# Transfers that sum weight blocks hang on ScalarE's convolutions, four raw weight buffers, first activations split in the up projection, six chunks held

## The chip, the cores and the metric

The kernel runs as one program on one core of a Trainium2 chip. The time is device microseconds (us) of one execution, and less is better. A difference between kernels is read from the medians of several executions; where a profile is discussed, the time of that one profiled execution is given beside its span, which runs from the first to the last instruction.

A core has five instruction streams that run side by side and wait for one another through semaphores: TensorE (PE; its weight loads are the row PEld), VectorE (DVE), ScalarE (ACT), GpSimd (POOL) and SyncE (SP). Each runs its instructions in order. Transfers are issued by SP, ACT or POOL, each with a queue of its own, and carried out by 16 DMA engines that all queues share. In the profile q1 is SP's queue, q10 ACT's and q0 POOL's.

## The reference

One layer of an encoder on x of 512 x 1024 float32, in three parts, each between two RMS norms and added to the residual: token mixing (an attention group and a recurrent group, HGRN2), cross-attention into 256 memory rows, and a gated MLP with a convolution over three neighbouring positions. Cut to what the change touches:

```python
def conv_ffn(h, w_up, conv_w, conv_b, w_down):
    n = h.shape[1]
    u = h @ w_up                                  # 512 x 1024 @ 1024 x 5632
    up = jnp.pad(u, ((0, 0), (1, 1), (0, 0)))
    acc = conv_b
    for j in range(3):
        acc = acc + up[:, j:j + n] * conv_w[j]
    gate, val = jnp.split(acc, 2, axis=-1)
    return (jax.nn.silu(gate) * val) @ w_down     # 512 x 2816 @ 2816 x 1024

h = rmsnorm(x, pre_ffn_g)
x = x + rmsnorm(conv_ffn(h, w_up, conv_w, conv_b, w_down), post_ffn_g)
```

## The kernel before

**Precision.** Every float32 operand is split into two parts of a shorter format: `hi`, a cast made by ScalarE, and `lo`, the rest, `source - hi`. A product is three matmuls (`mm3`, L176 to L178): hi by hi, hi by lo, lo by hi. For the weights the parts are `wh` and `wl`.

**Weights.** All weights but those of the down projection lie in DRAM as 110 units of 128 x 1024 (512 KB), in the order in which they are used. `load_w` (L132) takes the next of two buffers `raw` and lets SP load it (L136 for these units, L141 for the down projection's). `issue` (L145) then makes `wh` and `wl`, in four buffers each: normally by a cast on ScalarE (L111) and a subtraction on VectorE (L112). For 35 units of the first half, `wl` is made as a negated copy of `wh` (ScalarE L155 or POOL L157) to which POOL adds the weights by an accumulating transfer from DRAM (L158). Up to three units are issued ahead of the one in use (`AHEAD`). One unit serves 24 matmuls of 512 columns in a projection.

**Down projection.** It is a product of 2 x 2 blocks: tokens 0 to 255 and 256 to 511 against even and odd chunks of 128 features, by two halves of the output columns. Seven block products (`PRODUCTS`) take the place of eight; each has 11 chunks, two row blocks and three matmuls a chunk, so 66 matmuls of 512 columns, and reads 6 weight units (the last of half width). Three of its weight operands are blocks of `w_down` as they stand (`in_wd`: w11, w22, w21), the other four are sums of blocks (`SUMS`: t1, t3, t2, t4). The sums are made in DRAM by transfers alone: `new_sums` (L926) copies a block into a tensor `sum_t` (L930) and adds another to it by an accumulating transfer (L931). t2 is built on t1, and t4 on t2. There are six groups `u` of 1024 columns (the last 512), so 6 x 4 x 2 = 48 transfers, all on POOL's queue. The order of the products is w11, t2, t1, w22, t3, t4, w21.

The activations have sums too. `acts[g]` holds the gated activations of group `g` (chunks 0 to 3, 4 to 7, 8 to 10) as an even and an odd tile; `group_sides` (L934) makes the differences `sides[g]` and turns one half of the even tile into a difference, and `left_side` (L982) splits the operand of product `p` and group `g` into `hi` and `lo`. For group 1 of the products 1 to 6 (`NEG_GROUP`) `lo` is made by POOL and an accumulating transfer (L993, L994), otherwise by VectorE. `lay_ahead` keeps three groups prepared ahead (`LAY_AHEAD`).

**Large tiles.** `b8` is a pool of 16 tiles of 8 KB a partition, given out by `big`: x, the activations, the sides, the left sides and the gains (`gains`, L187) all come from it. A tile is handed to the next owner when its last reader is done.

**The up projection.** It runs over 22 feature blocks `i` and the two halves `c` (gate, value); `conv` (L943) computes the convolution of each: ScalarE L946, VectorE L947 and L949, SiLU on ScalarE (L952) for the gates, the gating product on VectorE (L957). `new_sums(u)` is called behind blocks 2, 5, 8, 11, 14 and 17.

**What sets the order.** The code is written in one sequence, and a scheduler then orders the instructions of each engine by priority and estimated readiness. An instruction that waits for nothing may so be ordered far ahead of its place in the code; `tc.issue_after(ins)` puts an instruction behind `ins` on the same engine. The order is fixed when the kernel is built.

**Start.** Four units against all of x (L407) come first while x and its transposed copy are loaded. ScalarE's squares of x (L420) give the row norms, POOL turns them into a power (L194, L195), and the units from L176 on follow. The recurrent group's output norm is again ScalarE, POOL L195, VectorE L593, PE L597.

Of the kernel before, what the change touches and what calls it, by code (L numbers as in the profile page):

```python
# [9 lines left out]
F32 = mybir.dt.float32  # L10
# [8 lines left out]
P = 128  # L19
# [15 lines left out]
NEG_GROUP = frozenset((p, 1) for p in range(1, 7))  # L35
# [45 lines left out]
def layer(tc, io, out):  # L81
# [49 lines left out]

    def load_w():  # L132
        raw = rawp.tile([P, 1024], F32, name="raw", tag="raw")
        i = issued[0]
        if i < N_WHOLE:
# [787 lines left out]
    acts, sides, gates = [], [], {}  # L923
    half_t = [slice(0, 256), slice(256, 512)]

    def new_sums(u):  # L926
        n = width(u).stop - width(u).start
        for out_name, first_name, second_name in SUMS:
            t = dram.tile([P, n], F32, name="sum_%s_%d" % (out_name, u), tag="sum_%s_%d" % (out_name, u))
            nc.gpsimd.dma_start(t, weight_block(first_name, width(u)))  # L930
# [11 lines left out]

    def conv(c, i, u):  # L943
# [36 lines left out]
    g_post, = gains("post_ffn_g")  # L980

    def left_side(p, g):  # L982
        n = GROUPS[g][1] - GROUPS[g][0]
        even, odd = acts[g]
        if p == 3:
            nc.vector.tensor_sub(sides[g][:, 1, :n], odd[:, :n, half_t[0]], sides[g][:, 1, :n])
        src = (even[:, :n, half_t[0]], sides[g][:, 1, :n], sides[g][:, 0, :n], sides[g][:, 1, :n],
               even[:, :n, half_t[1]], odd[:, :n, half_t[1]], odd[:, :n, half_t[0]])[p]
        t = big([P, 2, 4, 256], F32R)
        hi, lo = t[:, 0, :n], t[:, 1, :n]  # L990
        if (p, g) in NEG_GROUP:
            nc.scalar.copy(hi, src)  # L992
            nc.gpsimd.tensor_scalar(lo, hi.bitcast(F32), -1.0, 0.0, op0=ALU.mult, op1=ALU.add)  # L993
            nc.gpsimd.dma_start(lo, src, accum_op=ALU.add)  # L994
        else:
            split(hi, lo, src)
        return hi, lo

    order = [(p, g) for p in range(7) for g in range(3)]
    laid = {}  # L1000

    def lay_ahead(i):
        while len(laid) < min(len(order), i + LAY_AHEAD):
            laid[order[len(laid)]] = left_side(*order[len(laid)])
# [162 lines left out]
```

## Time and profile before

| | us |
|---|---|
| median of three executions (lowest, highest) | 923.49 (922.62, 924.53) |
| the profiled execution, its own time | 924.11 |
| its span | 922.3 |
| PE busy | 840.2, 91% of the span |
| VectorE busy | 533.1, 58% |
| ScalarE busy | 457.5, 50% |
| POOL busy | 143.6, 16% |

How to read the views: a group of instructions is named by line, engine, operation and `out<-in`, with buffer numbers left out. Behind `|` stands the idle time of the engine just before it, with what ended that idle time. In a timeline the columns are start, duration, engine, line, operation, and in brackets the idle time before it and its releaser. In the view of waits stand the engine and line that waited, what it waited for, the total in us, how often, and the longest. PE's matmuls are pipelined, so the spacing of their starts says more than their durations.

### The profile page before, as it was taken

How to read it: one execution, taken by the hardware profiler on the slowest of the kernel's cores; microseconds unless marked ns; L12 is line 12 of the kernel's file. 1: busy time of each engine (PE TensorE's matmuls, PEld its weight loads, DVE VectorE, ACT ScalarE, POOL GpSimd, SP SyncE). 2: the span in 40 equal slices, each digit the busy share in tenths (PEclk: the TensorE clock that was granted, in tenths of full speed). 3: DMA queues.
4: the chain of work that ended last, by engine and by line, in shares of the span. 5: the costliest groups of instructions: out<-in, count | busy, mean ns of one | idle time of the engine just before them, and what ended most of it. 6: DMA issues, size and time to landing. Idle time of an engine off the chain costs nothing.

```text
span 922.3 us, 11153 instructions
## 1 busy us (share of the span) xinstructions
PE 840.2 (91%) x4238; PEld 701.4 (76%) x4238; DVE 533.1 (58%) x800; ACT 457.5 (50%) x766; POOL 143.6 (16%) x209
## 2 busy tenths in 40 slices
PE   7683977999999999999999999999999996987884
PEld 5472766888989988888888898888888885865663
DVE  2232434773998677584453665556556557555554
ACT  3354355563879887464453554333433343454431
POOL 2141324111442320120000310000000000112011
PEclk9887898999999999999999999999999998999998
DMA  9999998746595763234222143232222332569453
GB/s 291 349 271 288 261 286 193 154 92 137 134 212 134 161 137 143 87 114 137 81 81 69 46 137 115 92 106 99 92 92 92 115 91 58 162 180 210 138 165 126
DMA packets 40198, 136.69 MB, mean 148 GB/s; under 512 B 5136, under 2 KB 7184, under 8 KB 39952
## 3 DMA queue, kind: packets, MB, share of 16 engines
q1 hardware_dynamic: 25632, 86.03, 27.5%
q0 software_dynamic: 13216, 47.19, 24.2%
q10 hardware_dynamic: 1296, 2.76, 0.8%
q8 instruction: 33, 0.54, 0.2%
q14 instruction: 21, 0.17, 0.1%
HBM read 130.72 MB, written 25.17 MB: 169 GB/s over the span
## 4 chain that ended last, share of the span: by engine, by line
PE 67%; DMA 16%; DVE 6%; issue 5%; POOL 3%; ACT 3%; SPq 0%; POOLq 0%; DVEq 0%; ACTq 0%
PE ps_b L178 8%; PE ps_b L177 7%; PE ps_b L176 7%; DMA sum_t<-in_wd_dram 5%; PE ps_s L176 4%; PE ps_s L178 4%; PE ps_s L177 4%; PE ps_o L176 4%; DMA raw<-sum_t 4%; PE ps_o L177 4%; PE ps_o L178 4%; PE ps_c L176 3%; PE ps_c L177 3%; PE ps_c L178 3%; DMA big<-in_x_dram 3%
## 5 line engine op out<-in xcount | busy, mean ns | idle before, releaser
L112 DVE TENSOR_TENSOR wl<-raw,wh 128x1024 fp32r<-128x1024 f32 (+1 forms) x113 | 134.3, 1190 | 177.5 <-ACT wh L111 177.2
L111 ACT CAST wh<-raw 128x1024 fp32r<-128x1024 f32 (+1 forms) x113 | 115.7, 1024 | 197.2 <-PE ps_b L177 53.3
L176 PE MATMUL ps_b<-big,wh 128*128 128x512 f32 (+1 forms) x320 | 120.2, 376 | 6.5 <-ACT wh L111 5.8
L178 PE MATMUL ps_b<-big,wl 128*128 128x512 f32 (+1 forms) x320 | 118.2, 369 | 0.0
L177 PE MATMUL ps_b<-big,wh 128*128 128x512 f32 (+1 forms) x320 | 117.9, 369 | 0.0
L176 PEld LDWEIGHTS ps_b<-big,wh 128*128 128x128 f32 x320 | 61.6, 192 | 16.2 <-ACT wh L111 6.2
L177 PE MATMUL ps_s<-wl,big 128*128 128x512 f32 (+1 forms) x140 | 55.7, 398 | 17.8 <-DMA wl<-in_w_dram 17.2
L178 PEld LDWEIGHTS ps_b<-big,wl 128*128 128x128 f32 x320 | 61.1, 191 | 10.4 <-DVE wl L112 0.8
L177 PEld LDWEIGHTS ps_b<-big,wh 128*128 128x128 f32 x320 | 61.5, 192 | 9.3
L569 DVE TENSOR_TENSOR big<-big 128x512 f32<-128x512 f32 x64 | 48.4, 761 | 32.9 <-PE ps_c L543 25.8
L176 PE MATMUL ps_s<-wh,big 128*128 128x512 f32 (+1 forms) x140 | 55.2, 398 | 2.0 <-ACT wh L111 1.6
L178 PE MATMUL ps_s<-wh,big 128*128 128x512 f32 (+1 forms) x140 | 55.1, 394 | 0.0
L993 POOL TENSOR_SCALAR big<-big 128x1024 fp32r<-128x1024 f32 x6 | 6.3, 1054 | 290.6 <-ACT big L992 290.6
L153 ACT CAST wh<-raw 128x1024 fp32r<-128x1024 f32 x35 | 36.8, 1050 | 27.5 <-PE ps_o L178 11.4
L177 PEld LDWEIGHTS ps_s<-wl,big 128*128 128x128 f32 x140 | 27.7, 198 | 24.0 <-DMA wl<-in_w_dram 18.1
L112 DVE TENSOR_TENSOR big<-ps_o,big 128x512 fp32r<-128x512 f32 x54 | 37.1, 688 | 13.4 <-ACT big L111 13.1
L176 PE MATMUL ps_b<-wh,big 128*128 128x512 f32 x92 | 38.7, 424 | 5.9 <-ACT wh L111 3.4
L178 PE MATMUL ps_b<-wh,big 128*128 128x512 f32 x92 | 38.0, 415 | 4.6 <-DVE big L112 4.6
L176 PE MATMUL ps_o<-wh,big 128*128 128x512 f32 (+1 forms) x102 | 39.5, 392 | 2.9 <-ACT wh L111 2.9
L158 POOL DMA_DIRECT2D wl<-in_w_dram x35 | 33.3, 969 | 54.2 <-ACT wl L155 38.3
L204 POOL TENSOR_SCALAR small<-small 128x1 f32<-128x1 f32 x41 | 17.9, 436 | 152.1 <-ACT tmp L235 133.0
L111 ACT CAST big<-ps_o 128x512 fp32r<-128x512 f32 x54 | 31.7, 587 | 19.4 <-PE ps_o L891 7.5
(266 smaller groups left out, 2074.8 us busy)
## 6 DMA issues: line engine op xcount, KB each, us to landing
raw<-in_w_dram SPq DMA_DIRECT2D x109, 512.0 KB, 3.2
wl<-in_w_dram POOLq DMA_DIRECT2D x35, 512.0 KB, 6.1
sum_t<-in_wd_dram POOLq DMA_DIRECT2D x30, 512.0 KB, 9.9
raw<-sum_t SPq DMA_DIRECT2D x20, 512.0 KB, 3.3
raw<-in_wd_dram SPq DMA_DIRECT2D x15, 512.0 KB, 4.0
sum_t<-sum_t POOLq DMA_DIRECT2D x10, 512.0 KB, 7.5
big<-in_x_dram SPq DMA_DIRECT2D x8, 512.0 KB, 14.7
big<-big POOLq DMA_DIRECT2D x6, 512.0 KB, 5.6
```

The lines of the kernel that those rows point to most:

```text
L111: nc.scalar.copy(hi, src)
L112: (eng or nc.vector).tensor_sub(lo, src, hi.bitcast(F32))
L153: nc.scalar.copy(wh, raw)
L158: nc.gpsimd.dma_start(wl, io["w"][i], accum_op=ALU.add)
L176: nc.tensor.matmul(o, a[0], b[0], start=start, stop=False)
L177: nc.tensor.matmul(o, a[0], b[1], start=False, stop=False)
L178: last_mm[0] = nc.tensor.matmul(o, a[1], b[0], start=False, stop=stop).ins
L204: nc.gpsimd.tensor_scalar(ss[:, i + 4:i + 5], ss[:, i:i + 1], 1.0 / D, ss[:, i + 3:i + 4] if i else EPS, op0=ALU.mult, op1=ALU.add)
L569: nc.vector.tensor_tensor(out=c, in0=c, in1=pat(tt, toff + off, [[2, npair], [gap, 2], [0, m]]), op=ALU.mult)
L993: nc.gpsimd.tensor_scalar(lo, hi.bitcast(F32), -1.0, 0.0, op0=ALU.mult, op1=ALU.add)
```

## The change

It has six parts.

1. In `new_sums`, the first transfer of t1 and of t3 (a plain copy of `in_wd`) is issued by ScalarE, and behind the last SiLU before it in the code (`last_act`). POOL keeps the copies for t2 and t4 and the 24 accumulating transfers.
2. `load_w` takes the down projection's units in turns of four: two into the buffers `raw`, two into the halves of a `big` tile (`raw_room`).
3. `left_side` and `lay_ahead` move ahead of `conv`; the split of product 0, group 0 is called behind the value half of block 8, and three groups are laid before `group_sides(2)`.
4. `NEG_GROUP` loses the products 1 and 3: VectorE makes `lo` of group 1 there.
5. The gains `post_ffn_g` are no tile of their own; they are read into the unused fourth chunk of group 2's tiles, and `out_part` takes the place of `residual_part` in the down projection.
6. `last = NP - 6`: of the last product six chunks, not four, are computed first for row block 0 and then for row block 1, so their four weight units are held.

```diff
-NEG_GROUP = frozenset((p, 1) for p in range(1, 7))
+NEG_GROUP = frozenset((p, 1) for p in (2, 4, 5, 6))
...
+    def raw_room(i):
+        k = (i - N_WHOLE) % 4
+        if i < N_WHOLE or k < 2:
+            return rawp.tile([P, 1024], F32, name="raw", tag="raw")
+        if k == 2:
+            spare[0] = big([P, 2, 1024])
+        return spare[0][:, k - 2, :]
...
-            nc.gpsimd.dma_start(t, weight_block(first_name, width(u)))
+            if first_name in sums:
+                nc.gpsimd.dma_start(t, weight_block(first_name, width(u)))
+            else:
+                with tc.issue_after(last_act[0]):
+                    nc.scalar.dma_start(t, weight_block(first_name, width(u)))
             nc.gpsimd.dma_start(t, weight_block(second_name, width(u)), accum_op=ALU.add)
...
-            nc.scalar.activation(a, a, ACT.Silu)
+            last_act[0] = nc.scalar.activation(a, a, ACT.Silu).ins
...
+                if i == 16:
+                    for c2 in range(2):
+                        nc.gpsimd.dma_start(acts[2][c2][:, 3, :], rows_bc(io["post_ffn_g"][half(c2)], 512))
...
-            if i % 8 == 7 or i == NF - 1:
+            if i % 8 == 7:
                 group_sides(i // 8)
+            if i == 8:
+                lay_ahead(1)
...
+    lay_ahead(3)
+    group_sides(2)
...
-    last = NP - 4
+    last = NP - 6
...
-                lay_ahead(3 * p + j // 4)
+                lay_ahead(3 * p + j // 4 + LAY_AHEAD)
```

**POOL at the start.** POOL's order before, a piece in the token mixing; `sum_t` are the sums with their group and number, L158 a remainder `wl`, L194 and L195 a row norm's power:

```order
L931 DMA sum_t_4_5764<-in_wd_dram 128x1024
L930 DMA sum_t_5_5992<-in_wd_dram 128x512
L930 DMA sum_t_5_5995<-in_wd_dram 128x512
L930 DMA sum_t_4_5767<-sum_t_4_5764 16x8192
L158 DMA wl<-in_w_dram 128x1024
L194 TENSOR_SCALAR small<-small 128x4
L931 DMA sum_t_5_5992<-in_wd_dram 128x512
L195 TENSOR_TENSOR small<-small,nhalf 128x4
```

The same piece of POOL's order now (the lines have moved by ten: L168, L204 and L205 are the old L158, L194 and L195):

```order
L205 TENSOR_TENSOR rx<-rx,nhalf 128x4
L462 CAST masks<-tmp_296 128x896
L168 DMA wl<-in_w_dram 128x1024 x8
L204 TENSOR_SCALAR small<-small 128x4
L205 TENSOR_TENSOR small<-small,nhalf 128x4
```

Before, all 48 sums stand between POOL's first instruction and the recurrent group's first output; now none does, and the orders of PE, ScalarE and SP are the same up to the up projection.

**POOL and ScalarE in the up projection.** POOL's order before, behind the last row norm of the cross-attention:

```order
L204 TENSOR_SCALAR small<-small 128x1 x2
L207 TENSOR_TENSOR small<-small,nhalf 128x1
L189 DMA big<-in_post_ffn_g_dram 128x1024
L993 TENSOR_SCALAR big<-big 128x1024
L994 DMA big<-big 128x1024
```

POOL's order now at that place, the whole of group 0 and the first transfer of group 1 (4840 is t1, 4843 t3, 4846 t2, 4849 t4):

```order
L217 TENSOR_TENSOR small<-small,nhalf 128x1
L945 DMA sum_t_0_4840<-in_wd_dram 128x1024
L945 DMA sum_t_0_4843<-in_wd_dram 128x1024
L941 DMA sum_t_0_4846<-sum_t_0_4840 16x8192
L945 DMA sum_t_0_4846<-in_wd_dram 128x1024
L941 DMA sum_t_0_4849<-sum_t_0_4846 16x8192
L945 DMA sum_t_0_4849<-in_wd_dram 128x1024
L945 DMA sum_t_1_5068<-in_wd_dram 128x1024
```

ScalarE's order now behind the SiLU of block 2 (L992), with the two plain copies L944 of group 0:

```order
L992 ACTIVATE tmp_4799<-tmp_4799 128x512
L944 DMA sum_t_0_4840<-in_wd_dram 128x1024
L986 ACTIVATE tmp_4835<-ps_s,cw 128x512
L944 DMA sum_t_0_4843<-in_wd_dram 128x1024
L111 CAST wh<-raw 128x1024 x2
```

The groups follow one another on POOL, each behind its copies on ScalarE; within a group four transfers form a chain (t1's addition, t2's copy, t2's addition, t4's copy).

**SP around the down projection.** SP's order before, where the weight units of the up projection end (L136) and those of the down projection begin (L141):

```order
L136 DMA raw<-in_w_dram 128x1024 x64
L141 DMA raw<-in_wd_dram 128x1024 x5
L141 DMA raw<-in_wd_dram 128x512
L141 DMA raw<-sum_t_0_4846 128x1024
L141 DMA raw<-sum_t_1_5074 128x1024
L141 DMA raw<-sum_t_2_5308 128x1024
```

SP's order now at the same place (L146 and L151 are the old L136 and L141; `big` is half of a spare tile):

```order
L146 DMA raw<-in_w_dram 128x1024 x58
L151 DMA big<-in_wd_dram 128x1024 x2
L146 DMA raw<-in_w_dram 128x1024 x6
L151 DMA raw<-in_wd_dram 128x1024 x3
L151 DMA raw<-in_wd_dram 128x512
L151 DMA big<-sum_t_0_4846 128x1024
L151 DMA big<-sum_t_1_5074 128x1024
L151 DMA raw<-sum_t_2_5311 128x1024
```

The third and fourth unit of the down projection are loaded ahead of six units of the up projection. Later in SP's order some loads into spare tiles stand ahead of loads into `raw` that are used before them, for example those of t4's first two groups between those of t3's.

More of the change, by code (lines that the diff above doesn't have):

```diff
@@ L130, in width @@
         return slice(u * 1024, min(u * 1024 + 1024, NP * 512))
+    spare = [None]
+    def raw_room(i):
[5 more added lines that the diff above has]
+        return spare[0][:, k - 2, :]
     def load_w():
-        raw = rawp.tile([P, 1024], F32, name="raw", tag="raw")
         i = issued[0]
+        raw = raw_room(i)
         if i < N_WHOLE:
@@ L978, in layer, with out_part @@
             new_sums(i // 3)
[L980 to L1004, printed above, removed]
+    def out_part(ss, y, i, cols, last, tag="ta"):
+        n = cols.stop - cols.start
+        yg = tmp2(tag=tag)[:, :n]
+        nc.scalar.activation(yg, y, ACT.Square, accum_out=ss[:, i:i + 1])
+        rstd_part(ss, i, last)
+        g0 = cols.start % 512
+        nc.vector.tensor_mul(yg, y, acts[2][cols.start // 512][:, 3, g0:g0 + n])
+        return yg, cols
+    lay_ahead(3)
+    group_sides(2)
     def products(y, p, j, w, b):
@@ L1047, in layer @@
                 nc.vector.tensor_add(c12, y[b], v2[b])
-                parts[b].append(residual_part(rows[b], c12, g_post, 0, half(1), False, "th"))
+                parts[b].append(out_part(rows[b], c12, 0, half(1), False, "th"))
         elif p == 4:
@@ L1052, in layer @@
                 nc.vector.tensor_add(v2[b], y[b], v2[b])
-                parts[2 + b].append(residual_part(rows[2 + b], v2[b], g_post, 0, half(1), False))
+                parts[2 + b].append(out_part(rows[2 + b], v2[b], 0, half(1), False))
         elif p == 5:
```

30 lines of the change are left out of this document (26 added, 4 removed).

## The prediction

> **What bounds the kernel now.** I read the busy time by stage first, cut where the other views change. Columns: stretch, its length, each engine's busy us and count, granted TensorE clock, DMA share, GB/s.
>
> ```profile
> core 0: us, PE busy (x) PEld busy (x) DVE busy (x) ACT busy (x) POOL busy (x), PEclk, DMA share, GB/s
> 0.00:48.40 48.40, 31.46 (x104) 23.66 (x104) 11.40 (x18) 16.93 (x27) 10.53 (x22) 0.89 0.99 322
> 48.40:143.00 94.60, 65.87 (x308) 53.36 (x308) 33.46 (x61) 41.47 (x65) 30.37 (x39) 0.82 0.99 269
> 143.00:770.00 627.00, 624.29 (x3363) 533.64 (x3364) 401.17 (x626) 335.42 (x593) 81.63 (x123) 1.00 0.42 116
> 770.00:908.00 138.00, 115.12 (x451) 88.31 (x450) 81.15 (x85) 62.09 (x75) 18.44 (x20) 0.93 0.56 159
> 908.00:922.30 14.30, 3.42 (x15) 2.46 (x14) 5.88 (x12) 1.63 (x6) 2.64 (x5) 0.74 0.20 74
> ```
>
> From 143 to 770 TensorE is busy 624.29 of 627 us: there is nothing to win there, only to lose. It idles 16.9 us before 48.4, 28.7 us up to 143 and 22.9 us in the down projection (770 to 908). In the two early stages the DMA engines are full (0.99). So I asked what PE waits for in the first 160 us, and what POOL waits for there (us in total, times, longest).
>
> ```profile
> PE ps_s L177 <- DMA wl<-in_w_dram: 17.2, 2, 11.0
> PE ps_c L597 <- DVE tmp L593: 11.0, 1, 11.0
> PE ps_s L407 <- ACT wh L383: 9.8, 3, 5.1
> PE ps_b L176 <- ACT wh L111: 5.8, 1, 5.8
> ...
> POOL sum_t L930 <- DMA sum_t<-in_wd_dram: 64.8, 11, 11.5
> ```
>
> POOL issues the weight remainders `wl` (L158) and computes the small power (L195), and it stands 64.8 us in front of transfers that only the down projection needs, 600 us later. Its timeline shows this at the last long wait:
>
> ```profile
> 138.73 0.51 POOL L930 DMA_DIRECT2D sum_t<-sum_t  x1 [9.94 <-DMA sum_t<-in_wd_dram]
> ...
> 141.12 1.39 POOL L195 TENSOR_TENSOR small<-small,nhalf 128x4 f32<-128x4 f32 x1
> ```
>
> L597's 11.0 us are this wait, since DVE L593 needs L195. Before 48.4 the sums take transfer time instead. The queues of 0 to 45 us (packets, MB, share of the 16 engines), two groups of issues (count, KB, median us to landing), and ScalarE's last square of x:
>
> ```profile
> q0 software_dynamic: 1633, 7.21, 57.4%
> q1 hardware_dynamic: 2316, 6.96, 41.2%
> ...
> sum_t<-in_wd_dram POOLq DMA_DIRECT2D x11, 512.0 KB, 9.7
> ...
> sum_t<-sum_t POOLq DMA_DIRECT2D x4, 512.0 KB, 6.8
> ...
> 46.29 1.06 ACT L420 ACTIVATE tmp<-big 128x1024 f32<-128x1024 f32 x1 [1.35 <-DMA big<-in_x_dram]
> ```
>
> In the down projection the bound is another: SP cannot issue a weight load before VectorE has released one of two raw buffers. SP's wait of 770 to 910, and PE's longest one there, at the stage's start:
>
> ```profile
> SPq L141 <- DVE wl L112: 90.4, 37, 11.9
> ```
>
> ```profile
> PE ps_b L178 <- DVE big L112: 4.6, 1, 4.6
> ```
>
> Two loads into one buffer that follow each other in the chain of work (start, us):
>
> ```profile
> 816.31 3.63 DMA raw<-sum_t
> ...
> 822.30 5.12 DMA raw<-sum_t
> ```
>
> One turn of a buffer (load 3.63, cast, subtraction) is 6.0 us, so 2.4 us beside the load; two buffers give a unit every 3.0 us, more where a load takes 5.1.
>
> **The change part by part**, against the profiled execution, 924.11 us (span 922.3 and 1.8 around it; the median of the runs, 923.49, is 0.6 lower, which I leave uncorrected).
>
> *Start, 0 to 48.4.* The changed order issues no sum there. What is left, q1's 6.96 MB, took 41.2% of 45 us, so 18.5 us of all engines; with some 4 us for issue and latency (estimated from the 3.63 of one load) x and the first weights are in by about 23 us instead of 46.3. Then PE's own 96 matmuls bind: 96 x 0.227 (the spacing below) is 22 us from its first at 5 us, and about 5 us more at the low clock: the stage ends near 32. **Gain 16.4**; bounds 8 (half the idle comes back) and 19 (the low clock costs half).
>
> *48.4 to 143.* POOL now holds `wl` issues and small operations alone, so the waits for `wl` (17.2) and L597's 11.0 go: with 0.5 of small ones the stage's 28.7. Each long wait also leaves the matmuls slow for a while:
>
> ```profile
> 93.62 0.80 PE L177 MATMUL ps_s<-wl,big 128*128 128x512 f32 x1 [10.96 <-DMA wl<-in_w_dram]
> ...
> 98.48 0.63 PE L176 MATMUL ps_o<-wh,big 128*128 128x512 f32 x1
> 98.91 0.43 PE L177 MATMUL ps_o<-wl,big 128*128 128x512 f32 x1
> 99.18 0.39 PE L178 MATMUL ps_o<-wh,big 128*128 128x512 f32 x1
> 99.41 0.40 PE L176 MATMUL ps_o<-wh,big 128*128 128x512 f32 x1
> ```
>
> For 5.3 us they start 0.43 apart, then 0.23: twelve matmuls lose 0.2 each, 2.4 us. For the four waits of 5.8, 6.2, 11.0 and 11.0 us I take 2 us each, 8 in all. Late next are the chain cast, negate, `wl` transfer and VectorE's recurrence, which now have 37 us less; I keep 5.7 us for them. **Gain 31**; bounds 20 and 37.
>
> *Up projection (inside 143 to 770).* Twelve plain copies are now issued by ScalarE and the other 36 transfers by POOL, which had nothing to do there. ScalarE's share is low enough (335 of 627 us) that twelve issues cost nothing; without that cover, 12 x 0.5 (the 0.51 of POOL's issue, the nearest row) is 6 us. A weight load now shares the engines. Its price, from a stretch where a load also ran beside POOL's transfers (260 to 340 us, medians again):
>
> ```profile
> wl<-in_w_dram POOLq DMA_DIRECT2D x13, 512.0 KB, 5.5
> raw<-in_w_dram SPq DMA_DIRECT2D x12, 512.0 KB, 3.2
> ```
>
> PE takes a unit each 24 x 0.227 = 5.45 us, two raw buffers allow a turn of 10.9, so a load may take 8.5 us before PE waits; 3.2 is far from it. I take **a loss of 2** for bunched transfers; bounds 0 and 20 (rival B). The first activations, split inside the up projection and not after it, save the stage's first wait (4.6, on the subtraction of that group, and 2.4 at the low clock) and cost a cast and a subtraction in covered time.
>
> *Down projection.* 7 products x 66 matmuls x 0.227 is 105 us. Busy is 115, so 10 are lost to the low clock and 22.9 idle. Four raw buffers halve the supply to 1.5 us a unit (at loads of 5.1: 1.9), below PE's 12 x 0.227 = 2.7, so PE becomes the bound. Late next: VectorE, with two more subtractions of two left sides (1 us each) and 81 of 138 us busy, would be near 75% of the shorter stage; and the two added buffers come from the pool of left sides, so SP's queue, in order, can stand before a slot that PE frees. For these I keep 9 of the 33 us. **Gain 24**; bounds 7 (A) and 33.
>
> Whether the 10 us follow the waits is weighed here. After a wait of only 1.6 us in this stage a matmul soon lasts 0.63 too, as in the slow stretch above:
>
> ```profile
> 854.48 0.73 PE L176 MATMUL ps_s<-wh,big 128*128 128x512 f32 x2 [1.58 <-ACT wh L111]
> ...
> 858.06 0.63 PE L176 MATMUL ps_s<-wh,big 128*128 128x512 f32 x1
> ```
>
> So I let short waits cause low clock, and it goes with them; the other reading is rival E. The Trainium skill, "TensorE: Matmul & The Clock Gate", section "Part 1: The HAM clock gate (the "warmup" mystery)", says that the clock falls after an idle window of about 3.4 us. By it only the stage's longest waits would lower the clock, and E would hold; this row disagrees.
>
> *End.* Six chunks instead of four are computed for one half before the other: 1.4 us more between the two tails, so the first tail no longer meets the second. The stage of 14.3 us is a chain; I take 0, bounds -1 and +2. The gains row read into spare activation slots changes one transfer in covered time: 0, bounds -1 and +1.
>
> Sum: 16.4 + 31 - 2 + 24 + 0 = 69.4; 924.1 - 69.4 = **855**.
>
> **The rivals.**
>
> A, *the end keeps its stalls*: slots of the pool come free no faster than PE works, and SP's order behind them makes the four buffers act as two. For it: loads into the new buffers stand in SP's queue ahead of loads needed sooner. Then only the first wait and its clock (7 of 33) are gained: 16.4 + 31 - 2 + 7 = 52, 872.
>
> B, *weight loads slow in the up projection.* Three queues now run at once on engines that one loads alone today. If a load took three times as long, 9.6 us, a turn would be 12.0 and a unit 6.0: 0.55 over PE's, times 36 units under the sums 20 us, 18 beyond the 2 above: 873. Against it: the 3.2 beside POOL's transfers. The Trainium skill, "DMA: Bandwidth & Descriptors", section "Queues, rings and completion order", has each DMA engine go round its queues packet by packet, which would make that threefold time the limit; the trace shows no doubling with one other queue.
>
> C, *the sums come late*, the one that ends slower. POOL now works one group's chain in a row: two adding transfers and two copies wait for one another, 2 x 9.7 + 2 x 6.8 and six issues of 0.5, 36 us a group at the full engines' medians. New groups come each 6 x 5.45 = 32.7 us; the last one at 770 - 8 x 5.45 = 726, and its second sum is needed near 800 less 8 for load and split. With c for a group, and 0.8c for the last group up to its second sum, PE waits 5 x (c - 32.7) + 0.8c - 66: from c = 40 on, and over 69 us, the whole gain, from c = 52 on. For it: 36 is near 40. Against it: those medians come from engines 99% taken. At c = 55 the time is 944.
>
> D, *the start frees less*: behind the sums stands the next wait (casts, the raw loads), and half of 47 comes: 878.
>
> E, *the down projection's low clock is not its short waits'*: then the wait of 4.6 us stands for 2.4 of the 10, and 7.6 stay: 863. Against it: the rows at 854 to 858.
>
> That the sums would still run early is ruled out by the order: they hang on the activations.
>
> **How the numbers follow.** Forecast 855 (838 to 868): 0.57. A 872 (866 to 884): 0.17. B 873 (864 to 895): 0.09. D 878: 0.07. E 863: 0.03. More than the forecast, all 14.7 us kept back regained, under 838: 0.04. C: 0.03. The range 838 to 884 takes in the forecast, A, E, most of B and D; its lower end is the sum with what is kept back regained. A measurement of this kernel tells 0.2% from no change: faster 0.96, same 0.01 (C near its break-even), slower 0.03.
>
> **What would show it.** Right: no sum on POOL before the up projection; no PE wait for `wl` or L593; the end of the first stage near 32 and L597 near 95; PE without waits in the up projection, with loads under 8.5 us; the down projection's 462 matmuls in about 114 us. Wrong: PE waiting on casts behind `raw` in the up projection (B), a wait for `sum_t` in the second product (C), SP waiting on PE in the down projection (A), or the early stages idle behind another engine (D).

## The result, and the profile after

| | before | after |
|---|---|---|
| median of four executions, us (lowest, highest) | 924.01 (922.62, 924.99) | 828.05 (826.70, 828.51) |
| ratio to before (95% interval) | | 0.896 (0.8944 to 0.8976) |
| the profiled execution, us (its span) | 924.11 (922.3) | 828.14 (826.4) |

The changed kernel is faster by 96.0 us in the profiled executions; 69.4 were forecast (855). The measured time lies below the forecast's range of 838 to 884. The direction and the stages were right, and so, for the most part, was what PE had waited for. The forecast gain was too small in every stage.

First the busy time by stage of the changed kernel, cut at the same places in the program as before: the end of the first stage, L607 (before L597), the up projection's last matmul and the down projection's last. Columns as in the prediction.

```profile
core 0: us, PE busy (x) PEld busy (x) DVE busy (x) ACT busy (x) POOL busy (x), PEclk, DMA share, GB/s
0.00:28.10 28.10, 26.54 (x105) 21.32 (x106) 15.16 (x27) 17.60 (x29) 2.40 (x9) 1.00 0.86 294
28.10:87.80 59.70, 58.37 (x310) 48.83 (x309) 31.48 (x58) 39.22 (x63) 10.43 (x15) 1.00 0.74 195
87.80:713.10 625.30, 622.61 (x3365) 532.41 (x3364) 401.61 (x624) 338.57 (x597) 101.28 (x150) 1.00 0.57 151
713.10:818.30 105.20, 105.12 (x464) 86.60 (x462) 81.97 (x89) 60.05 (x74) 15.96 (x18) 1.00 0.64 195
818.30:826.40 8.10, 0.28 (x2) 0.00 (x0) 3.66 (x8) 0.91 (x4) 1.34 (x3) 0.79 0.35 131
```

PE is now busy to within 3 us in each of the first four rows, and the clock column is 1.00 in all of them. The down projection's 105.12 us are what 462 matmuls take at the warm spacing of 0.227 (104.9): nothing is left of its waits or its low clock. VectorE is busy 82 of 105 us there, 78%, and PE loses nothing by it. The DMA share of the two early stages fell from 0.99 to 0.86 and 0.74; in the long middle row it rose from 0.42 to 0.57 without a cost.

The last two cuts of the kernel before, at the same places (the prediction had cut at 770 and 908; the wait before the first matmul is part of the stage):

```profile
770.10:911.10 141.00, 118.12 (x464) 90.67 (x463) 81.88 (x86) 62.81 (x77) 18.44 (x20) 0.93 0.55 155
911.10:922.30 11.20, 0.32 (x2) 0.00 (x0) 5.14 (x10) 0.91 (x4) 2.64 (x5) 0.66 0.25 94
```

So the gains by stage, in us:

| stage | before | after | gain | forecast (bounds) |
|---|---|---|---|---|
| first stage | 48.4 | 28.1 | 20.3 | 16.4 (8, 19) |
| up to L597 / L607 | 94.6 | 59.7 | 34.9 | 31 (20, 37), with the next row's part |
| from there to the down projection | 627.1 | 625.3 | 1.8 | -2 for the sums (-20, 0) |
| down projection | 141.0 | 105.2 | 35.8 | 24 (7, 33) |
| end | 11.2 | 8.1 | 3.1 | 0 (-1, +2) |

The 1.8 us of the third row are the slow matmuls behind L597's wait of 11 us, which the prediction had counted in the second stage; that stage's gain is 36.7. Between 188 and 770 us the distance of the two kernels stays at 57 us: the sums cost the up projection nothing.

PE's waits over the whole changed kernel (us in total, times, longest), the four largest:

```profile
PE ps_b L378 <- DVE tmp L359: 1.3, 1, 1.3
PE ps_s L187 <- DMA wl<-in_w_dram: 0.9, 1, 0.9
PE ps_b L186 <- DVE big L112: 0.8, 1, 0.8
PE ps_b L661 <- ACT big L662: 0.7, 2, 0.5
```

Of the 17.2 us for `wl` 0.9 are left, L607 does not stand here at all, and none of these waits lies in the up or the down projection. Transfers of the middle stretch (count, KB, median us to landing):

```profile
raw<-in_w_dram SPq DMA_DIRECT2D x93, 512.0 KB, 3.4
sum_t<-in_wd_dram POOLq DMA_DIRECT2D x20, 512.0 KB, 8.1
...
sum_t<-sum_t POOLq DMA_DIRECT2D x10, 512.0 KB, 4.6
```

A weight load takes 3.4 us, far from the 8.5 at which rival B would begin.

### The profile page after: what moved, and what is told of

Same layout as the page of the kernel before. It is cut to its first block, busy times and chain, and to the rows that moved or that the text cites. A ratio compares the mean times of both kernels' runs of the same rounds, so it can differ in the third digit from the quotient of the medians.

```text
span 826.4 us, 11158 instructions
## 1 busy us (share of the span) xinstructions
PE 812.9 (98%) x4238; PEld 689.2 (83%) x4238; DVE 533.9 (65%) x802; ACT 456.3 (55%) x766; POOL 131.4 (16%) x194
## 4 chain that ended last, share of the span: by engine, by line
PE 91%; DVE 3%; issue 2%; DMA 1%; ACT 1%; POOL 1%; POOLq 0%; DVEq 0%; ACTq 0%
PE ps_b L187 9%; PE ps_b L188 9%; PE ps_b L186 9%; PE ps_s L187 6%; PE ps_s L188 6%; PE ps_s L186 6%; PE ps_o L186 5%; PE ps_o L187 5%; PE ps_o L188 5%; PE ps_c L187 5%; PE ps_c L186 5%; PE ps_c L188 5%; PE ps_c L553 3%; PE ps_o L798 2%; PE ps_s L776 2%
## 5 line engine op out<-in xcount | busy, mean ns | idle before, releaser
L112 DVE TENSOR_TENSOR wl<-raw,wh 128x1024 fp32r<-128x1024 f32 (+1 forms) x93 | 112.2, 1208 | 117.5 <-ACT wh L111 117.3
L111 ACT CAST wh<-raw 128x1024 fp32r<-128x1024 f32 (+1 forms) x93 | 96.0, 1033 | 138.4 <-PE ps_b L187 44.0
L186 PE MATMUL ps_b<-big,wh 128*128 128x512 f32 (+1 forms) x320 | 118.2, 369 | 0.8 <-DVE big L112 0.8
L187 PE MATMUL ps_b<-big,wh 128*128 128x512 f32 (+1 forms) x320 | 116.4, 364 | 0.0
L579 DVE TENSOR_TENSOR big<-big 128x512 f32<-128x512 f32 x64 | 48.4, 761 | 16.3 <-PE ps_c L553 9.4
L186 PE MATMUL ps_s<-wh,big 128*128 128x512 f32 (+1 forms) x140 | 53.7, 384 | 0.4 <-DVE big L112 0.4
L188 PE MATMUL ps_s<-wh,big 128*128 128x512 f32 (+1 forms) x140 | 53.1, 379 | 0.0
L168 POOL DMA_DIRECT2D wl<-in_w_dram x35 | 30.7, 877 | 121.3 <-ACT wl L165 106.3
L945 POOL DMA_DIRECT2D sum_t<-in_wd_dram x24 | 19.6, 831 | 125.1 <-DMA sum_t<-in_wd_dram 76.1
L186 PE MATMUL ps_o<-wh,big 128*128 128x512 f32 (+1 forms) x102 | 39.4, 386 | 0.0
L992 ACT ACTIVATE tmp<-tmp 128x512 f32<-128x512 f32 x22 | 13.9, 632 | 44.7 <-DVE tmp L989 44.7
L187 PE MATMUL ps_o<-wl,big 128*128 128x512 f32 (+1 forms) x102 | 38.2, 375 | 0.0
L188 PE MATMUL ps_o<-wh,big 128*128 128x512 f32 (+1 forms) x102 | 38.2, 374 | 0.0
L186 PE MATMUL ps_b<-wh,big 128*128 128x512 f32 x92 | 36.9, 402 | 0.0
```

The lines of the kernel that those rows point to most:

```text
L112: (eng or nc.vector).tensor_sub(lo, src, hi.bitcast(F32))
L168: nc.gpsimd.dma_start(wl, io["w"][i], accum_op=ALU.add)
L186: nc.tensor.matmul(o, a[0], b[0], start=start, stop=False)
L187: nc.tensor.matmul(o, a[0], b[1], start=False, stop=False)
L188: last_mm[0] = nc.tensor.matmul(o, a[1], b[0], start=False, stop=stop).ins
L579: nc.vector.tensor_tensor(out=c, in0=c, in1=pat(tt, toff + off, [[2, npair], [gap, 2], [0, m]]), op=ALU.mult)
```

## The experiments

There are fifteen kernels. Times are medians. Ratios are to runs of the kernel before on the same chip, with 95% intervals where there are four executions. `...` marks what is left out of a code cut.

**Which parts bring what: the sums alone, and all but the sums.** Part 1 of the change alone, on the kernel before:

```diff
-            nc.gpsimd.dma_start(t, weight_block(first_name, width(u)))
+            if first_name in sums:
+                nc.gpsimd.dma_start(t, weight_block(first_name, width(u)))
+            else:
+                with tc.issue_after(last_act[0]):
+                    nc.scalar.dma_start(t, weight_block(first_name, width(u)))
...
-            nc.scalar.activation(a, a, ACT.Silu)
+            last_act[0] = nc.scalar.activation(a, a, ACT.Silu).ins
```

> The kernel before, with the sums hung on ScalarE's convolutions (part 1) and nothing else of the change. By the terms on record (16.4 + 31 - 2) it gains 45, so 879 us. By the trace of the changed kernel, where the first stage ended at 28.1 instead of 48.4 and everything up to the up projection stood 57.1 earlier, and if nothing but the sums did that, it gains 57: 867. If the parts help one another (POOL or the queues freed by the others), it lies between. In every case the down projection keeps its waits: about 141 us from its first matmul to its last, as before.

And the changed kernel with POOL issuing all copies again, behind nothing:

> The changed kernel, with all sums again issued by POOL and hung on nothing, so that they run at the start (part 1 undone). By the terms on record the rest gains 24: 900. By the trace of the changed kernel the down projection (105.1 us instead of 140.9) and the end (8.2 instead of 11.3) gain 38.8 by themselves: 885. If the down projection's gain needs the sums out of the way too, more than 885. The early stages should be as in the kernel before: the first stage's end near 48, the up projection's end at about 770.

Measured: 864.11 us (0.9341, 0.9323 to 0.9358) and 886.52 (0.9584, 0.9564 to 0.9604). Against the runs of before beside them (925.2) the gains are 61.1 and 38.7, together 99.8; the whole change has 96. By stage, the sums alone:

```profile
0.00:27.60 27.60, 26.21 (x104) 20.69 (x105) 14.45 (x26) 17.84 (x29) 2.03 (x9) 1.00 0.85 293
27.60:87.00 59.40, 58.47 (x310) 48.89 (x310) 32.25 (x59) 39.27 (x63) 11.17 (x15) 1.00 0.76 199
...
712.20:852.40 140.20, 119.15 (x464) 89.41 (x462) 81.81 (x86) 62.77 (x77) 18.68 (x20) 0.93 0.55 156
```

and all but the sums:

```profile
48.10:142.40 94.30, 66.19 (x308) 53.61 (x309) 33.40 (x61) 41.47 (x65) 30.46 (x39) 0.83 1.00 270
...
769.40:874.40 105.00, 104.89 (x464) 86.51 (x462) 81.84 (x89) 60.10 (x74) 15.36 (x18) 1.00 0.64 195
```

The two halves of the change hardly touch each other (98.4 us together in the profiled executions, against 95.9): with the sums alone the early stages are those of the changed kernel and the down projection that of before; with the rest alone it is the other way round. The estimate from the trace (867 and 885) holds to 3 us, the terms on record (879 and 900) are 15 and 13.5 too slow. So the early terms are the sums' alone, and the down projection's is the others' alone.

**What the early sums cost: the engines' time, or POOL standing.** Twelve plain copies that nobody reads, as POOL's first transfers, and in a second kernel behind the first row norm's power:

```diff
+    def spare_copies():
+        for n in range(12):
+            t = dram.tile([P, 1024], F32, name="extra_%d" % n, tag="extra_%d" % n)
+            nc.gpsimd.dma_start(t, io["wd"][n % 4][:, width(n // 4)])
...
```

> The changed kernel with 12 more plain copies of 512 KB of weight blocks into DRAM tensors that nobody reads, issued by POOL as its first transfers. They wait for nothing, so POOL stands before none of them; only the engines are shared. Theory T (in the first stage the sums took transfer time): 6.3 MB at the rate of q0 before (7.21 MB in 57.4% of 45 us) are 22 us of all engines, beside 18.5 for the loads: x and the first weights are in by 41 and the first stage ends near 42 instead of 28, +14, 842 us (838 to 850). Theory P (it was POOL's queue that stood): no wait on POOL, so +0 to 1: 828 to 829.

> The changed kernel with the same 12 copies that nobody reads, issued by POOL behind the first row norm's power (near 24 us), so in the second stage. Theory P (there the cost was POOL standing before transfers that wait for one another): POOL stands before nothing, 12 issues of 0.5 us delay the first remainder once, +0 to 3: 828 to 831. Theory T (the transfers' own time): the stage leaves a quarter of 60 us of the engines idle and the copies want 22, remainders land later while they run: +7 to 15, 835 to 843.

Measured: 839.35 and 839.88 (two executions each), 11 to 12 us over the changed kernel (10 to 11 by the ratios). One point of the expectations was wrong: behind eight copies POOL waited for the first to land before it issued the ninth, some 6 to 8 us in all. It did not decide. In the first kernel the first stage ends at 38.7 instead of 28.1, while POOL's next work, the row norm's power, waits for ScalarE anyway. The stage, and POOL's queue in it (packets, MB, share of the 16 engines):

```profile
0.00:38.70 38.70, 29.72 (x104) 22.46 (x104) 11.42 (x19) 17.04 (x27) 8.08 (x20) 0.91 0.96 369
...
q0 software_dynamic: 1728, 6.29, 41.5%
```

The copies bring back 10.6 of the stage's 20.3 us. They took less time for each MB than the sums did: 41.5% of 38.7 us for 6.29 MB, 2.6 us of all engines a MB, where the sums before, six of 15 of them additions, took 57.4% of 45 us for 7.21 MB, 3.6 a MB. Whether the additions make this difference was not tried.

In the second PE has one long wait more. ScalarE's cast and negation that come before the `wl` it waits for, in this kernel (start, us):

```profile
48.63 1.04 ACT L163 CAST wh<-raw 128x1024 fp32r<-128x1024 f32 x1 [4.36 <-DMA raw<-in_w_dram]
50.11 1.04 ACT L165 ACTIVATE wl<-wh 128x1024 fp32r<-128x1024 f32 x1
```

The `wl` was issued at 51.45 and used at 55.01, after PE had waited 9.4 us. In the changed kernel the same cast starts at 40.87. It is the raw load that was late (ScalarE waited 4.4 us for it): theory T, in the second stage too.

The other half of the question, POOL taken without a transfer added:

```diff
-            nc.gpsimd.dma_start(wl, io["w"][i], accum_op=ALU.add)
+            ins = nc.gpsimd.dma_start(wl, io["w"][i], accum_op=ALU.add).ins
+            busy[0] += 1
+            for _ in range(2 if busy[0] <= 8 else 0):
+                with tc.issue_after(ins):
+                    ins = nc.gpsimd.tensor_tensor(out=scratch, in0=scratch, in1=nhalf, op=ALU.pow).ins
...
```

> The changed kernel with POOL kept busy behind each of the first eight remainders by two powers of 128x16 (an estimated 3.2 us each, from 1.04 at four columns and 1.76 at eight), about what it stood for each remainder before (some 60 us over eight), with no transfer added. Theory P (POOL's standing costs by itself): issues of remainders can follow each other only every 7.5 us, where the changed kernel has 3 to 9; the eighth is some 10 us later, and the recurrent group's norm waits too: +8 to 20, 836 to 848. Theory T (only the engines' time counted): 828 to 830.

Measured: 835.45 (two executions), 7.4 over the changed kernel and just under what theory P expected. PE's waits up to 100 us:

```profile
PE ps_c L614 <- DVE tmp L610: 3.6, 1, 3.6
PE ps_s L191 <- DMA wl<-in_w_dram: 2.5, 1, 2.5
```

These are the two places of the prediction (L610 is the old L593, behind POOL's power), at a smaller price: 51 us of POOL's time cost 7.4 (in the kernel before POOL stood 60.6 us before sums in this stage). So both mechanisms are real; that the engines' time is the larger rests on an estimate. The second stage moved 25.4 MB before (269 GB/s x 94.6 us) and 11.6 after; 13.8 MB at the price of the copies (11.8 us for 6.3 MB) are 26 us, an estimate, beside 7 for POOL; the stage gained 36.7. Whether the price grows in step with the MB, and how the rest divides, was not tried.

**The down projection: two raw buffers.** `raw_room` gives a tile of `rawp` for every unit:

```diff
-        k = (i - N_WHOLE) % 4
-        if i < N_WHOLE or k < 2:
-            return rawp.tile([P, 1024], F32, name="raw", tag="raw")
-        if k == 2:
-            spare[0] = big([P, 2, 1024])
-        return spare[0][:, k - 2, :]
+        return rawp.tile([P, 1024], F32, name="raw", tag="raw")
```

> The changed kernel with two raw weight buffers in the down projection (part 2 undone). By the terms on record two buffers leave all of that stage's gain but its first wait (7 of 33) undone: 828 + 26 = 854. In the run of the sums alone, whose down projection is that of before, 2.5 + 4.1 of PE's idle time lay at the stage's start and some 14 in waits for casts and subtractions later, and it lasted 140: if only the start is saved, the stage takes about 131, so 828 + 26 again. Rival: the early split saves nothing while loads are late anyway: 828 + 35 = 863. Rival: the buffers were not the bound, the splits were: under 835.

Measured: 855.70 us (two executions), and the stage:

```profile
712.90:844.00 131.10, 114.06 (x464) 85.75 (x462) 81.14 (x85) 59.84 (x74) 17.21 (x16) 0.99 0.55 159
```

131.1 us, as expected: the two buffers are worth 26 of the 35.8, 17 us of idle time (131.1 less 114.1 busy) and 9 of busy time (114.1 against 105.1). Little of the 9 is low clock: the granted clock is 0.99, and only 7 matmuls start 0.43 apart, 1.4 us. The rest lies in slower restarts behind waits and in gaps that the profile does not list as waits. So waits of up to 2.0 us came back here almost without low clock.

**The first splits: the early call, and the order of the calls.** Two kernels: without the early call, and also with the last group's differences ahead of the first splits as before.

```diff
-            if i == 8:
-                lay_ahead(1)
```

```diff
-            if i % 8 == 7:
+            if i % 8 == 7 or i == NF - 1:
                 group_sides(i // 8)
-            if i == 8:
-                lay_ahead(1)
...
     lay_ahead(3)
-    group_sides(2)
```

> The changed kernel without the early split of product 0, group 0 (part 3 undone but for the order of the calls). By the term on record the first wait (4.6) and its low clock (2.4) come back: 835. By the run of the sums alone (2.5 + 4.1 idle at the stage's start, and the low clock behind them) 837. Rival: with three groups laid before the last differences are made, VectorE reaches that split in time anyway: 828 to 830.

> The changed kernel without the early split and with the last group's differences (VectorE, three operations) ahead of the first splits again, as before (the whole of part 3 undone). The run without the early split alone was no slower, so if the order of these calls is what saves the first wait, it comes back here: 2.5 + 4.1 of idle time as in the run of the sums alone, and 0 to 2.4 of low clock: 834 to 837. If the four buffers or the lead of the loads save it, 828.

Measured: 827.40 (0.8965, 0.8945 to 0.8984) and 838.42 (0.9064, 0.9014 to 0.9115). The early call is worth nothing that can be measured: the scheduler moves the split ahead by itself (VectorE makes it at 657.11, inside the up projection). The order of the calls is worth 10 us. VectorE in the second kernel, at the stage's start:

```profile
716.48 0.96 DVE L953 TENSOR_TENSOR big<-big 128x768 f32<-128x768 f32 x1
717.47 0.96 DVE L954 TENSOR_TENSOR big<-big 128x768 f32<-128x768 f32 x1
718.35 0.95 DVE L955 TENSOR_TENSOR big<-big 128x768 f32<-128x768 f32 x1
719.21 3.22 DVE L112 TENSOR_TENSOR big<-big 128x1024 fp32r<-128x1024 f32 x3
```

and PE:

```profile
714.68 0.50 PE L186 MATMUL ps_b<-wh,big 128*128 128x512 f32 x1 [2.52 <-ACT big L111]
720.48 1.22 PE L188 MATMUL ps_b<-wh,big 128*128 128x512 f32 x2 [4.61 <-DVE big L112]
```

Three differences that only the third group needs stand in front of the first split, and PE waits until that split is done. These are the waits that stood in the kernel before, 7.1 us together, with low clock behind them; the stage takes 117.3 us.

**How much room the down projection has: VectorE's load, and parts 4 and 5.** Every third subtraction done twice; `NEG_GROUP` as before; the gains in a tile of their own:

```diff
             split(wh, wl, raw)
+            if i >= N_WHOLE and i % 3 == 0:
+                nc.vector.tensor_sub(wl, raw, wh.bitcast(F32))
```

> The changed kernel with every third subtraction of a weight unit in the down projection done twice (14 of 42; 1.2 us each, 17 us more on VectorE, 82 + 17 = 99 of the stage's 105 us). If VectorE's load in this stage costs PE time from about 75% on, as the 9 us kept back on record supposed, over 9 us: 838 or more. If PE stays the bound as long as a unit's turn over four buffers (about 4.5 + 2.4 + 1.2 us, so 2.0 a unit) is under PE's 2.7: 828 to 830.

> The changed kernel with NEG_GROUP as before (part 4 undone): VectorE loses two subtractions of 1.2 us, POOL and its accumulating transfer make those two left sides again. If VectorE's load was worth keeping time back for, it is faster: 826 or less. If PE is the bound whatever VectorE does, 828. If the transfer (7.9 us to landing in the down projection, and 36 us of the sums ahead of it in POOL's queue at the stage's start) is late or holds a slot that SP waits for, slower: 831 to 840.

> The changed kernel with the gains in a tile of their own again (part 5 undone): of the 16 large tiles one less is left for left sides and spare raw buffers in the down projection. By the term on record 0, within 1: 827 to 829. By rival A's mechanism (SP's queue stands before a slot, loads needed sooner stand behind it) the missing tile makes SP stand longer: 832 or more, and PE waits on casts in the products 3 to 6.

Measured: 832.74 (0.9004, 0.8970 to 0.9038; executions from 828.4 to 835.8), 829.78 (0.8986, 0.8967 to 0.9004) and 829.97 (0.8990, 0.8967 to 0.9012). The last two intervals overlap that of the changed kernel (0.8944 to 0.8976); in their profiles the down projection is 2.0 and 1.0 us longer, as their first-to-last matmuls show (107.2 and 106.2 against 105.1). With more work on VectorE the executions run from 828.4, as the second expectation has it, up to 835.8; none reached the 838 of the first, and the interval overlaps that of the changed kernel. The chain of work in its profiled execution, the longest (835.78):

```profile
767.98 7.47 DMA raw<-sum_t
775.53 1.05 ACT wh L111
776.61 1.24 DVE wl L112
777.87 1.24 DVE wl L172
```

PE waits 1.65 and 2.02 us for this unit, and the clock falls. The last row is the added subtraction itself, which stands between the unit and PE here. The load was issued only at 767.98, because SP stood before the load into a spare tile ahead of it. SP's waits there, 750 to 800 us:

```profile
SPq L151 <- DMA big<-big: 7.1, 1, 7.1
```

The tile belonged to a left side whose accumulating transfer was not done; in the changed kernel the same wait is 2.4, and with the gains in a tile of their own 10.4, where PE waits 0.8 us in the whole stage. That is rival A's mechanism, SP's order behind a slot. It is there, and in the changed kernel PE does not wait for it.

**The end: four chunks held.** `last = NP - 4` again.

> The changed kernel with four chunks of the last product held, not six (part 6 undone). By the term on record 0: 828, at most 829. By the two traces: before, VectorE reached the last addition 2.9 us behind the start of the last matmul, since the first half's tail stood in front of it; in the changed kernel 0.6. If that is part 6, 2.3 us come back: 830.3.

Measured: 828.37 (0.8972, 0.8956 to 0.8988), no difference that can be told. In the profile the last addition comes 2.0 us behind the last matmul's start (816.60 to 818.60; 0.6 in the changed kernel), but the stretch of matmuls is 0.4 shorter. Of the end's 3.1 us about 1 is part 6. With two raw buffers, six chunks held, the end takes 10.4 us, with four buffers and four chunks held 9.4: so 2.3 of the 3.1 hang on the four buffers. That this is because the last weights are there in time is argued, not shown.

**When the sums would be late.** A group behind the blocks 11, 13, ... 21:

```diff
-        if i % 3 == 2 and i // 3 < 6:
-            new_sums(i // 3)
+        if i % 2 and i >= 11:
+            new_sums((i - 11) // 2)
```

> The changed kernel with the sums later and closer: a group behind the blocks 11, 13, 15, 17, 19 and 21 (21.8 us apart, from about 603 us on) instead of 2, 5, ... 17. POOL's chain of a group sets the pace, c, and the second product needs the last group's t2 in DRAM by about 736. With c near 30, the spacing of the trace with loads beside it, t2 of the last group is there at 603 + 5 x 30 + 12 = 765: PE waits 29, 857 us. With the c = 36 of rival C it is there at 798: 890. If the sums were not on PE's path at all (rival C without a price): 828.

Measured: 863.25 (two executions). PE's waits from 712 us on begin with

```profile
PE ps_s L186 <- ACT wh L111: 28.6, 2, 14.6
```

28.6 us, all in the second product, against the 29 worked out from c = 30; the rest of the 35 us over the changed kernel are waits behind it and the low clock. Rival C's mechanism is as it was told; its price of 36 us a group was taken from full engines and was too high. In the changed kernel POOL issues its last sum at 694.2, and the first unit of t2 is loaded at 715.6.

**Short waits and the clock.** Two kernels stop PE for known times in the up projection, by copies of activations onto themselves on ScalarE:

```diff
+    def stall(n):
+        hi = hT.hi[1][:, 3, :64]
+        ins = nc.scalar.copy(hi, hi.bitcast(F32)).ins
+        hi = hT.hi[0][:, 0:2, :]
+        for _ in range(n):
+            with tc.issue_after(ins):
+                ins = nc.scalar.copy(hi, hi.bitcast(F32)).ins
+        hi = hT.hi[0][:, 0, :64]
+        with tc.issue_after(ins):
+            nc.scalar.copy(hi, hi.bitcast(F32))
...
```

> The changed kernel with PE stopped once at every second block of the up projection, 21.8 us apart: ScalarE copies a part of the activations onto itself behind the last matmul of a block, and PE's next matmul reads it. The stops are about 0.8, 1.9, 2.9, 4, 5, 7 and 9 us, then three more of 0.8. Theory S (on record: a wait of 1.6 us is enough for low clock): from 1.9 us on every stop is followed by some 12 matmuls that start 0.43 apart instead of 0.23, 2 to 2.4 us each. Theory L (only long waits lower the clock): the stops up to 2.9 us are followed by none. In both the time is 828 plus about 33 of stops and 8 to 14 of low clock: 869 to 875; the spacing of the matmuls decides.

> The same stops behind every half block (5.45 us apart): 18 of 0.8 us from block 4 to 12, then 18 of about 2.9 us. Theory S: the second lot keeps the clock low for most of the 24 matmuls between two stops, 2 to 5 us for each stop beside the stop itself: 828 + 14 + 52 + 36 to 90, so 930 to 985; the first lot (0.8 each) leaves the clock high. Theory L: no slow matmuls anywhere: 828 + 14 + 52 = 894. If idle time counts as a share over some stretch and not wait by wait, the second lot is slow (2.9 of 8.4 us idle) and the first (0.8 of 6.3) is not, though the same 2.9 once by itself (the other kernel) may leave the clock high.

Measured: 890.61 and 989.85 (one execution each). The stops came out at 1.1 to 10.6 us in the first, since casts of weights stood between the copies, and at 1.87 and 4.0 to 4.4 in the second. Two stops of 1.87 us in a row, from the second kernel:

```profile
526.67 0.50 PE L186 MATMUL ps_s<-big,wh 128*128 128x512 f32 x1 [1.87 <-ACT big L1028]
527.00 0.39 PE L187 MATMUL ps_s<-big,wh 128*128 128x512 f32 x1
...
534.27 0.50 PE L186 MATMUL ps_c<-big,wh 128*128 128x512 f32 x1 [1.87 <-ACT big L1028]
...
535.40 0.63 PE L187 MATMUL ps_c<-big,wh 128*128 128x512 f32 x1
535.83 0.63 PE L188 MATMUL ps_c<-big,wl 128*128 128x512 f32 x1
...
538.72 0.39 PE L186 MATMUL ps_c<-big,wh 128*128 128x512 f32 x1
```

The first changes nothing; behind the second eight matmuls start 0.43 apart and PE loses 1.7 us. Of the 18 stops of 1.87 seven are followed by low clock, of those of 4.0 to 4.4 all fifteen that the trace has; in the first kernel every stop from 2.9 us on, and none of those of 1.2 and 1.9. A stretch of low clock costs 1.5 to 2.8 us, counted from the first matmul behind the stop, and it does not grow with the stop: 1.7 behind 2.94, 2.7 behind 4.02, 1.9 behind 10.57. So neither theory holds as it was put: a wait of 1.6 us can lower the clock, as the prediction had it, but does not always.

## Where the prediction was right, and which step of it failed

The mechanisms were mostly right; the sizes were not. The step that failed is the time set aside in each stage's sum for things that might be late next: 5.7 us in the second stage, 9 in the down projection, 2 in the up projection, and 5 us of low clock in the first. In their place the changed kernel shows about 1.3 us of waits in the second stage, none in the down and the up projection, and about 1 us of low clock in the first stage. Two smaller terms were mis-sized too: what the down projection had to give (33 for 35.6) and the end (0 for 3.1). The forecast fell short by 3.9 + 5.7 + 2 + 11.8 + 3.1 = 26.5 us, stage by stage:

- **First stage** (16.4, bounds 8 and 19; 20.3). Mechanism right: the sums took transfer time. Of the working, 96 x 0.227 = 22 us from PE's first matmul at 5 holds; "about 5 us more at the low clock" was the error. Five matmuls start slowly, some 1 us, as in the kernel before, whose own first rows I had not read for this: its slow matmuls stood mostly behind the later waits. With them gone nothing stands in the place of the transfers (rival D): the stage ends at 28.1.
- **Second stage** (31; 36.7). The sum before its deduction, 28.7 idle and 8 for the low clock, is 36.7, as measured; in part this is luck, since 27.4 of idle time and 9.3 of busy time went. The 5.7 kept back for "the chain cast, negate, `wl` transfer and VectorE's recurrence" were worked out from no row; PE waits about 1.3 us for them. The cause was named too narrowly: I laid the waits to POOL standing, and the runs show that the engines' time which the sums took costs as well, by the estimate above more (12 us for 6.3 MB, against 7 for 51 us of POOL).
- **Up projection** (-2; 0). Loads at 3.4 us, no wait. Rivals B and C did not come. B was not tried beyond this. C was: with c = 30 its chain puts the wait of the kernel with late sums at 29 us, and 28.6 were measured.
- **Down projection** (24; 35.8). Two errors. The 33 were too few: the 105 us of 462 matmuls were set against the busy 115.12 of a stretch with 451. For 451 the warm time is 102.4, so 12.7, not 10, us of busy time lay above it, and 35.6 were to be had. (The 12.7 are not all low clock: by the spacing of the matmuls about 7.4 are, and the rest are short gaps and slow restarts. All of it went.) And the 9 us kept back "for VectorE's load and SP's order behind slots" did not stay. That reserve came from a busy share (75%), not from an instruction that would be late. The runs show that its mechanism exists: 15 us more on VectorE (97.3 busy in a stage of 112.9), or one tile less, and SP's wait for a slot reaches 7 to 10 us. In the changed kernel that wait is 2.4, and PE waits for nothing in the stage.
- **First activations** (7 of these us). Near in size, wrong in place: the order of the calls saves the wait (2.5 and 4.6 us, 10 with what follows), the early call nothing.
- **End** (0; 3.1). "The first tail no longer meets the second" was seen and then priced at nothing. Part 6 by itself is about 1 us; the others hang on the four buffers.
- **Low clock follows the waits** (rival E at 0.03). Right as far as this kernel goes: with the waits the low clock went too, all of it (granted clock 1.00), so E did not come. But a short wait alone does not bring it: in the kernel with two raw buffers waits of 1.0 to 2.0 us came back, and only one of them is followed by low clock, 1.4 us.
- **Gains and `NEG_GROUP`** (0, and a load). Each is worth 1 to 2 us of the down projection's length; in time this is at the edge of what can be told.

What the failed terms have in common is the way they were made: 16.7 us kept back in three stages, another 4 in the first, each for something that might be late next and none worked out from a row. "All kept back regained" got a chance of 0.04, as if these were independent accidents; they were one assumption, that PE would not be the bound.

## What to carry to other kernels

Where a stage has one engine with nearly enough work to fill it, work out that engine's own time at its warm rate, from the count of all its instructions between the stage's real ends; that is the forecast once its waits go, and every deduction needs an instruction of the trace that will be late, with its time. Transfers that wait for nothing are ordered to the start by a scheduler and cost there twice, by the engines' time and by the queue that they stand in; hang them on something in a stretch whose DMA share is low. When a change brings several edits, undo them one at a time: here an order of calls is worth 10 us, and the early call beside it nothing.

## What the runs showed of the hardware

- **The full clock comes back on a grid.** In the kernel with a train of stops the matmuls become fast again at 538.72, 555.76, 572.80, 596.79, 613.86, 630.91 and 654.65 us: 17.04, 17.04, 23.99, 17.07, 17.05 and 23.74 apart, near 5 and 7 times 3.41, though the stops before the first three lie 16.8 apart. Of all periods from 2.5 to 8 us, 3.41 fits best the ends of the 23 slow stretches of this kernel (three or more matmuls 0.43 apart, from 300 us on), and of the 11 in the kernel before; for the six of the kernel with single stops 3.82 fits nearly as well. It fits that a stop of 1.87 us matters only by where it falls; that a stretch is judged by its share of idle time is argued, not shown. The Trainium skill, "TensorE: Matmul & The Clock Gate", section "Part 1: The HAM clock gate (the "warmup" mystery)", has a free-running window of 3413 ns, and the grid agrees; it has the clock fall after at least one idle window of about 3.4 us, and the rows above disagree: 1.87 us were enough in 7 of 18 stops.
- **Eight transfers, then a wait.** POOL issued eight independent copies in 4.3 us and the ninth only when the first had landed (in both kernels with extra copies). Whether the program's semaphores or the queue set this was not tried.
- **Full engines delay the loads.** With 6.3 MB of copies at the start, the loads of x took a median of 14.9 us to land and raw weights 11.3 in the first stage (DMA share 0.96), against 6.3 and 4.6 in the first stage of the changed kernel (0.86).
